# Hybrid DeltaNet and attention layer: compact diagonal blocks, unit blocks set by GpSimd, X stored in two parts, separate places for the out weights, later planned landings

## The chip, the cores and the metric

The kernel runs on one NeuronCore of a Trainium2 chip. The core has five engines with a queue each, which run in order and wait for one another by semaphores: TensorE (PE, with its weight loads shown as PEld), VectorE (DVE), ScalarE (ACT), GpSimd (POOL) and SyncE (SP), from which this kernel issues all its DMA transfers. The metric is the device time of one execution, in microseconds; less is better.

## What is computed

One layer of an encoder over 2048 positions of width 1024. The normalised input is projected once; the columns are split between a bidirectional gated DeltaNet of 4 heads of 128 and windowed attention of 8 query heads of 64. Both results are joined, multiplied by the output weights and added to the input. The DeltaNet part, cut to what the change touches:

```python
k_beta = k * beta[..., None]
m = jnp.where(strict, jnp.einsum('bhncd,bhnsd->bhncs', k_beta, k) * decay, 0.0)
eye = jnp.eye(c, dtype=q.dtype)
t_inv = lax.linalg.triangular_solve(eye + m, jnp.broadcast_to(eye, m.shape),
                                    left_side=True, lower=True, unit_diagonal=True)
u = jnp.einsum('bhncs,bhnse->bhnce', t_inv, v * beta[..., None])
w = jnp.einsum('bhncs,bhnsd->bhncd', t_inv, k_beta * jnp.exp(g)[..., None])
a_intra = jnp.where(incl, jnp.einsum('bhncd,bhnsd->bhncs', q, k) * decay, 0.0)
...
fwd = gated_delta_rule_chunked(q, k, v, g[:, :, 0], beta[:, :, 0])
bwd = flip(gated_delta_rule_chunked(flip(q), flip(k), flip(v), flip(g[:, :, 1]), flip(beta[:, :, 1])))
...
mix = jnp.concatenate([dn, sw], axis=-1).astype(x.dtype)
x = x + mix @ w_out[l].astype(x.dtype)
```

The kernel works with 16 chunks of 128 positions, where the reference has 32 of 64; the result is the same. All is in float32; the large products are made of three float32r products of a high and a low part.

## The kernel before

**Phase A** (`phase_a`) projects the input. For the second half of the positions it holds the x blocks 2 and 3 in the pools `xp0` and `xp1` and ends with the gates z (matmuls `pf_z`, first of block 2, then of block 3). Its pools stand on the right side of the on-chip memory in the order bp, xp0, xp1, wp, zp. Intermediate results go to DRAM tiles: `kq_d`, `v_d`, `zdn_d`, `mix_sw`.

**Phase B** (`phase_b`) runs the DeltaNet heads 0 to 3 one after the other, each in four steps.

1. `pre_front(h)`, by groups of four chunks (in the order 1, 2, 0, 3): k and q are loaded (L619) and transposed; `gh` (L656) is k·k and q·k. For both directions d, DVE multiplies by beta and the decay (L665) into `ma` [128, 4, 2, 128]: index 0 of the third axis is M (the strict triangle), index 1 is the intra-chunk matrix A. Both go in one DMA of 512 KB to the DRAM tile `m_d` (L670). POOL adds the two directions' M to `wm` (L672, called W below), which holds the lower triangle of one direction and the upper of the other.
2. `pre_back(h)`, first part: the 32x32 diagonal blocks of M of both directions (16 chunks, 4 blocks each, 128 blocks in all, one on each partition) are read from `m_d` into `L0` and `L` (L697, L698); `X` is loaded with unit blocks from the input `eye32` (L699). DVE turns L0 into L (L700) and inverts the blocks in 31 steps of two small operations (L704, L708), which is called the solve. X is stored to `x_d` in one DMA (L709).
3. `pre_back(h)`, second part: `spread` loads X by groups (`xc`, L757), transposes it (L758) and writes it with `own` as block-diagonal matrices `ut` and `tt` (L761, DVE and POOL). Products with `wm` (`za`, `ra`, `zb`, `rb`, L720) complete the inverse in `tt`.
4. `scan(h)`: 16 steps in each direction. A step loads `at` (A, from `m_d`, L781) and `kqc` (L784), and its chain is pk (L785), r (L787), py (L793), yk (L798), pn (L802), the new state S (L805). The output of a step is py times `at` and the like (L811). After step 12 and at the end `post` normalises, gates and stores to `mix_dn`.

In program order `pre_front(1)`, then scan 0, `pre_back(1)`, `pre_front(2)`, scan 1, and so on. Between them stand the matmuls of the attention half of the output projection (`out_half` with names in s, `pcs`, L566 to L568), which depend only on `mix_sw` and on the lower half of the output weights. Their result is stored to `part_d`. The upper half of the weights is loaded after scan 3, for the matmuls `pcd`, which add `part_d` and x (`xr`, `x2`, L561 to L570) and write the output.

`load_wo` loads a half of the output weights in eight pieces of 256 KB to a staging tile (L542), makes the high part on ACT (L543) and the low part on DVE (L544). Before the change both halves use the same tiles `woh` and `wol` of the pool `ww`. Staging tiles have the tag "ws" with two buffers, which `out_half` also uses. The pools of phase B on the right side stand in the order kv1, tp0, wo, ww, tp1, rp, kv2, over the places of bp, xp0, xp1 and wp; a pool may be used when all users of the places under it are done.

**The order of the work** is not that of the program. `set_order` takes all instructions, gives each a duration (`cost`) and each DMA a time to landing (`landing`), plans the queues of all five engines by list scheduling, forwards and backwards, tries 120 changed orders, and fixes the best by its own estimate. So any changed instruction or estimate gives a new order for the whole kernel, and each engine keeps to it, also where a transfer lands later than planned.

Of the kernel before, what the change touches and what calls it, by code (L numbers as in the profile page):

```python
# [8 lines left out]
F32 = mybir.dt.float32  # L9
# [7 lines left out]
P = 128  # L17
# [12 lines left out]
def tile_hybrid(ctx, tc, t, out, dbg=None):  # L30
# [16 lines left out]
    nw = const("nw", [P, KC], t["nwt"])  # L47
    bd = const("bd", [P, NCH, 16])
# [8 lines left out]
    with ExitStack() as ca:  # L57
        consts = phase_a(ca, tc, t, ident, nw, bd, gp, mix_sw, kq_d, v_d, zdn_d, zsw_d, dp)
# [6 lines left out]
def phase_a(ctx, tc, t, ident, nw, bd, gp, mix_sw, kq_d, v_d, zdn_d, zsw_d, q_pool):  # L65
# [15 lines left out]
    def const(name, shape, src=None):  # L81
        a = ap.tile(shape, F32, tag=name, name=name)
        if src is not None:
            dma(a, src)
        return a

    cw = gp.tile([P, 12, 5], F32, tag="cw", name="cw")
    dma(cw, t["cw"])
# [8 lines left out]
    edge = gp.tile([P, 12, 4], F32, tag="edge", name="edge")  # L97
# [420 lines left out]
def phase_b(ctx, tc, t, ident, consts, hp, mix_dn, mix_sw, kq_d, v_d, zdn_d, zsw_d, dp, out):  # L518
# [28 lines left out]
    def out_half(pool, bank, w, mx, srcs, dst, name, nb):  # L547
# [36 lines left out]
    with tc.using_default_side("right"):  # L584
        right = {n: pool(n, 2 if n == "wo" else 1) for n in 'kv1 tp0 wo ww'.split()}
    late = ctx.enter_context(ExitStack())
    with tc.using_default_side("right"):
        ps_s = pool("ps_s", stack=late, space=PSUM)
        right.update({n: pool(n, 2 if n == "rp" else 1, late) for n in 'tp1 rp kv2'.split()})
    kvp += [right["kv1"], right["kv2"]]  # L590
    tp = [right["tp0"], right["tp1"]]
    wo, ww, rp = right["wo"], right["ww"], right["rp"]
# [10 lines left out]
    def pre_front(h):  # L603
# [9 lines left out]
        m_d = dp.tile([2, NCH, 4 * (64 * P + 32)], F32, tag=f"m_d{h}", name=f"m_d{h}")  # L613
        x_d = dp.tile([2, NCH, P, 32], F32, tag="x_d", name=f"x_d{h}", bufs=2)
        for n, c4 in enumerate(FRONT):
# [53 lines left out]
            for d in range(2):  # L669
                dma(m_d[d, s4, : 2 * P * P].rearrange("u (i y) -> i u y", y=2 * P), mas[d].rearrange("p u a n -> p u (a n)"))  # L670
            wm[c4] = qp.tile([P, 4, P], F32, tag="wm", name=f"wm{h}_{c4}", bufs=7)
            G.tensor_tensor(wm[c4], mas[0][:, :, 0], mas[1][:, :, 0], ALU.add)  # L672
            tr = ps_t.tile([P, 4, P], F32, tag="tr", name=f"trv{h}_{c4}")
# [9 lines left out]
        H["solve"] = m_d, x_d  # L683
        return H

    def pre_back(h, H):
        wm, tt = H["wm"], H.setdefault("tt", {})
        m_d, x_d = H["solve"]
# [6 lines left out]
        lv = [m_d[d].rearrange("u (p y) -> (u p) y", p=4)[:, : 64 * P] for d in range(2)]  # L695
        lv = [a.rearrange("q (r x) -> q r x", x=2 * P)[:, :, :32] for a in lv]
        dma(L0, lv[0])  # L697
        dma(L[64:128], lv[1])  # L698
        dma(X, t["eye32"].partition_broadcast(P))  # L699
# [9 lines left out]
        dma(x_d.rearrange("d u (p r) c -> (d u p) (r c)", p=4), X.rearrange("p r c -> p (r c)"))  # L709
# [57 lines left out]
    def scan(h, H, rp, ps_s):  # L767
        ks, vs, ck, tt = (H[k] for k in ("ks", "vs", "ck", "tt"))
        m_d = H["solve"][0]
        oacc = H["oacc"] = {}  # L770
        st = {}
        for i in range(NCH):
            for d in range(2):
# [7 lines left out]
                dma(at, m_d[d, c, : 2 * P * P].rearrange("(i a j) -> i a j", a=2, j=P)[:, 1])  # L781
# [75 lines left out]
    ws = load_wo(wo, 4, "s")  # L857
# [35 lines left out]
def set_order(tc):  # L893
# [367 lines left out]
```

## Time and profile before

| | us |
|---|---|
| runs of before (3) | 1288.22, 1292.0, 1293.46 |
| median | 1292.0 |
| the profiled execution, its own time | 1291.88 |
| its span, first to last instruction | 1290.1 |
| head 0: solve, first step to store of X | 757 to 800 |
| head 1: solve | 847 to 913 |
| head 2: solve | 946 to 1016 |
| head 3: solve | 1043 to 1084 |
| scans 0 to 3, first S to last S | 837 to 920, 945 to 1031, 1049 to 1130, 1122 to 1201 |
| attention half of the output, first to last pcs | 805 to 1143 |
| last half of the output, first to last pcd | 1183 to 1286 |

The stages overlap: while one head is scanned, DVE solves the next one and PE runs the front of the one after. The profile is that of one execution, and all times in it count from its first instruction. Its rows are shown below, where they are used.

### The profile page before, as it was taken

The page shows a single profiled execution, that of the slowest core. Times are in us where ns is not written, and L with a number is a line of the kernel's source. Part 1 is how long each engine was busy: PE and PEld are TensorE (multiplying, and loading weights), DVE is VectorE, ACT ScalarE, POOL GpSimd, SP SyncE. Part 2 cuts the span into 40 slices and gives each one's busy share as a digit, 9 for nine tenths or more (in the row PEclk, how much of TensorE's full clock was granted, in tenths as well). Part 3 has the DMA queues.
Part 4 walks back from the last instruction along what each step waited for, and adds up shares of the span by engine and source line. Part 5 has one row for each costly group of instructions (what it writes and reads, how often), then busy time and mean ns, then how long its engine had stood idle before and what let it go on. Part 6 is the DMA issues. An engine that isn't in the chain of part 4 may idle for free.

```text
span 1290.1 us, 22274 instructions
## 1 busy us (share of the span) xinstructions
PE 1220.2 (95%) x7034; PEld 1043.6 (81%) x7034; DVE 939.1 (73%) x2346; ACT 700.8 (54%) x2057; POOL 486.3 (38%) x606
## 2 busy tenths in 40 slices
PE   4999999999999999999999999699999999998998
PEld 4998878888899987787778877587788788986776
DVE  4312477777888778799997878789779888766443
ACT  5322254435677777877755455476566655555211
POOL 1330214104667677886312313512422320213333
PEclk9999999999999999999999999799999999999999
DMA  8453244325542344421247567878868765378897
GB/s 259 129 144 104 82 145 146 119 86 173 162 123 81 113 117 135 137 88 67 74 146 265 177 175 240 221 190 256 236 158 255 248 160 159 100 230 272 250 309 227
DMA packets 238519, 218.01 MB, mean 169 GB/s; under 512 B 50624, under 2 KB 189632, under 8 KB 238400
## 3 DMA queue, kind: packets, MB, share of 16 engines
q1 hardware_dynamic: 238400, 216.58, 55.4%
q8 instruction: 56, 0.92, 0.3%
q14 instruction: 63, 0.52, 0.1%
HBM read 143.05 MB, written 73.47 MB: 168 GB/s over the span
## 4 chain that ended last, share of the span: by engine, by line
PE 75%; DMA 10%; DVE 6%; ACT 4%; issue 2%; SPq 2%; POOL 1%; DVEq 0%; ACTq 0%; POOLq 0%
PE pf_c L188 6%; PE pf_c L189 6%; PE pf_c L190 6%; PE pf_z L189 3%; PE pf_z L188 3%; PE pf_z L190 3%; PE pt L362 3%; PE pq_q L199 2%; PE pq_q L200 2%; PE pq_q L201 2%; PE pcs L566 2%; PE pcd L567 2%; PE gh L656 2%; PE pcs L567 2%; PE pk L793 2%
## 5 line engine op out<-in xcount | busy, mean ns | idle before, releaser
L239 DVE SCALAR_TENSOR_TENSOR acc<-pf_c,cw,acc 128x512 f32<-128x512 f32 (+2 forms) x192 | 140.6, 745 | 28.1 <-ACT acc L235 22.7
L188 PE MATMUL pf_c<-xhi,wh_c 128*128 128x512 f32 x384 | 150.8, 401 | 1.1 <-DVE acc L239 0.9
L189 PE MATMUL pf_c<-xlo,wh_c 128*128 128x512 f32 x384 | 151.6, 401 | 0.0
L190 PE MATMUL pf_c<-xhi,wl_c 128*128 128x512 f32 x384 | 149.5, 400 | 0.0
L357 POOL TENSOR_SCALAR pr<-pr,st 128x384 f32<-128x384 f32 (+1 forms) x128 | 84.6, 681 | 62.9 <-DVE st L355 32.4
L189 PE MATMUL pf_z<-xlo,wh_z 128*128 128x512 f32 x256 | 100.3, 404 | 0.0
L188 PE MATMUL pf_z<-xhi,wh_z 128*128 128x512 f32 x256 | 99.9, 404 | 0.0
L190 PE MATMUL pf_z<-xhi,wl_z 128*128 128x512 f32 x256 | 99.7, 402 | 0.0
L348 ACT ACTIVATE pr<-pr,st 128x384 f32<-128x384 f32 (+1 forms) x128 | 76.1, 596 | 21.3 <-DVE st L347 18.2
L188 PEld LDWEIGHTS pf_c<-xhi,wh_c 128*128 128x128 f32 x384 | 72.3, 188 | 16.8 <-DVE acc L239 1.6
L189 PEld LDWEIGHTS pf_c<-xlo,wh_c 128*128 128x128 f32 x384 | 72.2, 188 | 14.7
L190 PEld LDWEIGHTS pf_c<-xhi,wl_c 128*128 128x128 f32 x384 | 72.1, 188 | 14.5
L367 DVE TENSOR_TENSOR pl<-pt,ph 128x512 fp32r<-128x512 f32 x92 | 62.2, 685 | 23.2 <-ACT ph L366 22.4
L563 POOL TENSOR_TENSOR xrd<-xrd,x2d 128x512 f32<-128x512 f32 x32 | 42.3, 1324 | 95.9 <-DMA x2d<-x 35.3
L343 DVE CUSTOM_DVE_ANT_0 pr<-s,mask,sink 128x384 f32<-128x384 f32 (+1 forms) x128 | 73.4, 593 | 6.4 <-PE s L342 4.5
L362 PE MATMUL pt<-ident,pr 128*128 128x128 f32 x368 | 71.0, 275 | 2.3 <-POOL pr L357 1.0
L366 ACT ACTIVATE ph<-pt 128x512 fp32r<-128x512 f32 x92 | 53.7, 594 | 33.5 <-PE pt L362 27.1
L199 PE MATMUL pq_q<-wh_q,xhi 128*128 128x256 f32 x256 | 69.0, 289 | 0.8 <-ACT sgq L258 0.8
L200 PE MATMUL pq_q<-wh_q,xlo 128*128 128x256 f32 x256 | 69.5, 285 | 0.0
L201 PE MATMUL pq_q<-wl_q,xhi 128*128 128x256 f32 x256 | 68.2, 284 | 0.0
L798 ACT ACTIVATE yk<-pk,ck 128x128 f32<-128x128 f32 x120 | 44.1, 368 | 38.8 <-PE pk L793 38.1
L566 PE MATMUL pcs<-wohs,mhs 128*128 128x512 f32 x128 | 57.5, 449 | 6.0 <-ACT wohs L543 4.2
(251 smaller groups left out, 3775.1 us busy)
## 6 DMA issues: line engine op xcount, KB each, us to landing
m_d<-ma SPq DMA_DIRECT2D x32, 512.0 KB, 4.9
kqc<-kq_d SPq DMA_DIRECT2D x120, 128.0 KB, 3.3
ws_c<-wt SPq DMA_DIRECT2D x48, 256.0 KB, 3.4
xr<-x SPq DMA_DIRECT2D x16, 512.0 KB, 5.9
ws_z<-wt SPq DMA_DIRECT2D x32, 256.0 KB, 3.7
kq<-kq_d SPq DMA_DIRECT2D x16, 512.0 KB, 5.5
at<-m_d SPq DMA_DIRECT2D x128, 64.0 KB, 2.9
part<-xrs SPq DMA_DIRECT2D x32, 256.0 KB, 3.2
```

What stands on the lines that cost most here:

```text
L188: T.matmul(ps, hi[:, k, cs], xhi[b][:, k], start=(k == 0), stop=False)
L189: T.matmul(ps, hi[:, k, cs], xlo[b][:, k], start=False, stop=False)
L190: T.matmul(ps, lo[:, k, cs], xhi[b][:, k], start=False, stop=(k == KC - 1))
L199: T.matmul(ps[:, :n], xh, hi[:, k, :n], start=(k == 0), stop=False)
L200: T.matmul(ps[:, :n], xl, hi[:, k, :n], start=False, stop=False)
L201: T.matmul(ps[:, :n], xh, lo[:, k, :n], start=False, stop=(k == KC - 1))
L239: V.scalar_tensor_tensor(av, ps[:, lo:], cw[:, i, k : k + 1], av, ALU.mult, ALU.add)
L343: V.tensor_tensor_reduce(pr[j][:, :n], ps[:, :n], mask[:, lo * P : hi * P], 1.0, sink[:, hh : hh + 1], ALU.add, ALU.max, accum_out=mx[:, j ...
L348: A.activation(pr[j][:, :n], pr[j][:, :n], AF.Exp, bias=nm[:, j : j + 1], accum_out=den[:, j : j + 1])
L357: G.tensor_scalar(pr[j][:, :n], pr[j][:, :n], den[:, j : j + 1], 1.0, ALU.mult, ALU.mult)
L362: T.transpose(pt[:, j], pr[j][:, (kb - lo) * P : (kb - lo + 1) * P], ident)
L566: T.matmul(ps, mh[:, k], wh[:, k, ns], start=(k == 0), stop=False)
```

## The change

- `pre_front`: only A goes to DRAM, to the tile `a_d` (256 KB a DMA in place of 512). W is made by POOL as before; then four ACT copies take its four diagonal 32x32 blocks to `lc` [128, 4, 32], which is stored compactly to `l_d` (64 KB a group).
- `pre_back`: L0 and L are both read from `l_d`, 4 KB in a row for each partition, where they were 32 rows of 128 bytes each from `m_d`. Each reads both triangles and the solve uses one. The unit blocks are set by two memsets on POOL; the input `eye32` is gone. X is stored in two DMAs, rows 0 to 23 and rows 24 to 31 of each block.
- `scan`: `at` is read from `a_d`.
- Pools: on the right side now kv1, wo, wwh, wwl, tp0, then tp1, rp, kv2. The high and the low part of the first half of the weights have a pool each. Their staging goes round five buffers of `wo` (tags ws, ml, ws, ml, mh). The second half has its own pool `op`, on the left side after `pre_stack` is closed, and its load stands before scan 3 in program order. `oc`, with the buffers of the last output stage, moves to the right side after `wo`, `wwh`, `wwl` and `tp0` are closed; x2 has four buffers in place of two.
- The constants nw, bd, cw and edge, used in phase A only, go to a pool of phase A.
- `set_order`: issues of `at` and `kqc` are planned with 630 ns (450 or 560 before), and every DMA lands 700 ns later in the plan.

```diff
-    def load_wo(pool, k0, name, tg=""):
-        wh = ww.tile([P, 4, D], F32R, tag="woh" + tg, name=f"woh{name}", bufs=1)
-        wl = ww.tile([P, 4, D], F32R, tag="wol" + tg, name=f"wol{name}", bufs=1)
+    def load_wo(pools, k0, name, stage):
+        wh, wl = (p.tile([P, 4, D], F32R, tag=n, name=f"{n}{name}", bufs=1) for p, n in zip(pools, ("woh", "wol")))
...
-                sw = pool.tile([P, 512], F32, tag="ws", name=f"wos{name}_{k}_{j}")
+                sw = stage(2 * k + j)
...
-                x2 = pool.tile([P, 512], F32, tag="x2", name=f"x2{name}_{j}", bufs=2)
+                x2 = pool.tile([P, 512], F32, tag="x2", name=f"x2{name}_{j}", bufs=4)
...
-        right = {n: pool(n, 2 if n == "wo" else 1) for n in 'kv1 tp0 wo ww'.split()}
+        kvp.append(pool("kv1"))
+        outs = ctx.enter_context(ExitStack())
+        wo = pool("wo", 2, outs)
+        ww = [pool(n, stack=outs) for n in ("wwh", "wwl")]
+        tp = [pool("tp0", stack=outs)]
...
-        m_d = dp.tile([2, NCH, 4 * (64 * P + 32)], F32, tag=f"m_d{h}", name=f"m_d{h}")
+        l_d = dp.tile([NCH, P, 32], F32, tag="l_d", name=f"l_d{h}", bufs=2)
+        a_d = H["a_d"] = dp.tile([2, NCH, P, P], F32, tag=f"a_d{h}", name=f"a_d{h}")
...
-                dma(m_d[d, s4, : 2 * P * P].rearrange("u (i y) -> i u y", y=2 * P), mas[d].rearrange("p u a n -> p u (a n)"))
+                dma(a_d[d, s4].rearrange("u i y -> i u y"), mas[d][:, :, 1])
             wm[c4] = qp.tile([P, 4, P], F32, tag="wm", name=f"wm{h}_{c4}", bufs=7)
             G.tensor_tensor(wm[c4], mas[0][:, :, 0], mas[1][:, :, 0], ALU.add)
+            lc = qp.tile([P, 4, 32], F32, tag="lc", name=f"lc{h}_{c4}", bufs=2)
+            for q in quads:
+                A.activation(lc[q], wm[c4][q, :, q], AF.Copy)
+            dma(l_d[s4].rearrange("u i c -> i u c"), lc)
...
-        lv = [m_d[d].rearrange("u (p y) -> (u p) y", p=4)[:, : 64 * P] for d in range(2)]
-        lv = [a.rearrange("q (r x) -> q r x", x=2 * P)[:, :, :32] for a in lv]
-        dma(L0, lv[0])
-        dma(L[64:128], lv[1])
-        dma(X, t["eye32"].partition_broadcast(P))
+        lv = l_d.rearrange("u (p r) c -> (u p) r c", p=4)
+        dma(L0, lv)
+        dma(L[64:128], lv)
+        xf = X.rearrange("p r c -> p (r c)")
+        G.memset(xf, 0.0)
+        G.memset(xf[:, ::33], 1.0)
...
-        dma(x_d.rearrange("d u (p r) c -> (d u p) (r c)", p=4), X.rearrange("p r c -> p (r c)"))
+        xs = x_d.rearrange("d u (p r) c -> (d u p) r c", p=4)
+        for rs in (slice(0, 24), slice(24, 32)):
+            dma(xs[:, rs], X[:, rs])
...
-                dma(at, m_d[d, c, : 2 * P * P].rearrange("(i a j) -> i a j", a=2, j=P)[:, 1])
+                dma(at, H["a_d"][d, c])
...
-    ws = load_wo(wo, 4, "s")
+    def stage(i):
+        tag, bufs = (("ws", 2), ("ml", 2), ("ws", 2), ("ml", 2), ("mh", 1))[i % 5]
+        return wo.tile([P, 512], F32, tag=tag, name=f"wos{i}", bufs=bufs)
+
+    ws = load_wo(ww, 4, "s", stage)
...
     ps3 = pool("ps3", space=PSUM)
+    op = pool("op")
+    with tc.high_priority(-1000000):
+        w = load_wo((op, op), 0, "d", lambda i: op.tile([P, 512], F32, tag="wt", name=f"wod{i}", bufs=2))
     scan(3, H, rp3, ps3)
     late.close()
+    outs.close()
     with tc.using_default_side("right"):
         ps_c = pool("ps_c", 4, space=PSUM)
-    oc = pool("oc", 8)
-    with tc.high_priority(-1000000):
-        w = load_wo(wo, 0, "d")
+        oc = pool("oc", 8)
...
-            return 450 if dims < 2 else 560
+            return 630 if o[0].tensor.name.startswith(("at", "kqc")) else 450 if dims < 2 else 560
...
-            return 1800 + n / (450 if sum(c > 1 for _, c in o.ap) < 3 else 190)
+            return 2500 + n / (450 if sum(c > 1 for _, c in o.ap) < 3 else 190)
...
-        return 1900 + n / 190 + 1000 * any(t == 0 for t, _ in a.ap) + 1200 * (run < 64)
+        return 2600 + n / 190 + 1000 * any(t == 0 for t, _ in a.ap) + 1200 * (run < 64)
```

More of the change, by code (lines that the diff above doesn't have):

```diff
@@ L57, in tile_hybrid @@
     with ExitStack() as ca:
-        consts = phase_a(ca, tc, t, ident, nw, bd, gp, mix_sw, kq_d, v_d, zdn_d, zsw_d, dp)
+        consts = phase_a(ca, tc, t, ident, gp, mix_sw, kq_d, v_d, zdn_d, zsw_d, dp)
     with ExitStack() as cb:
@@ L62, in tile_hybrid, with phase_a @@
         dbg(tc, locals())
-def phase_a(ctx, tc, t, ident, nw, bd, gp, mix_sw, kq_d, v_d, zdn_d, zsw_d, q_pool):
+def phase_a(ctx, tc, t, ident, gp, mix_sw, kq_d, v_d, zdn_d, zsw_d, q_pool):
     nc = tc.nc
@@ L79, in phase_a, with const @@
     pso = ctx.enter_context(tc.tile_pool(reuse_waits="tile", name="pso", bufs=1, space=PSUM))
-    def const(name, shape, src=None):
-        a = ap.tile(shape, F32, tag=name, name=name)
+    def const(name, shape, src=None, pool=ap):
+        a = pool.tile(shape, F32, tag=name, name=name)
         if src is not None:
@@ L85, in const @@
         return a
-    cw = gp.tile([P, 12, 5], F32, tag="cw", name="cw")
-    dma(cw, t["cw"])
+    nw = const("nw", [P, KC], t["nwt"], zp)
+    bd = const("bd", [P, NCH, 16], None, zp)
+    cw = const("cw", [P, 12, 5], t["cw"], zp)
     mask = const("mask", [P, 3 * P], t["smask"])
@@ L96, in phase_a @@
     sink = const("sink", [P, NQ], t["sinks"].partition_broadcast(P))
-    edge = gp.tile([P, 12, 4], F32, tag="edge", name="edge")
+    edge = const("edge", [P, 12, 4], None, zp)
     half_neg = const("half_neg", [P, 16])
@@ L588, in phase_b @@
         ps_s = pool("ps_s", stack=late, space=PSUM)
[L589 to L592, printed above, removed]
+        tp.append(pool("tp1", stack=late))
+        rp = pool("rp", 2, late)
+        kvp.append(pool("kv2", stack=late))
     XE = V
@@ L681, in pre_front @@
             V.tensor_tensor(ck[:, d], bp[:, d], ekd[:, d, :, h], ALU.mult)
-        H["solve"] = m_d, x_d
+        H["solve"] = l_d, x_d
         return H
@@ L687, in pre_back @@
         wm, tt = H["wm"], H.setdefault("tt", {})
-        m_d, x_d = H["solve"]
+        l_d, x_d = H["solve"]
         L0 = qp.tile([P, 32, 32], F32, tag="kq", name=f"L0{h}", bufs=2)[:64]
```

5 lines of the change are left out of this document (1 added, 4 removed).

## The prediction

> **What bounds the kernel now.** I read the page first, then the busy time of each engine by stage (stages cut at the first and last instruction of each head's solve and scan), then the SP queue's timeline, the DMA issues, the waits and the chain that ended last.
>
> ```profile
> span 1290.1 us, 22274 instructions
> PE 1220.2 (95%) x7034; PEld 1043.6 (81%) x7034; DVE 939.1 (73%) x2346; ACT 700.8 (54%) x2057; POOL 486.3 (38%) x606
> ```
>
> PE looks full, and the change takes no matmul away. So all that can be won is time in which PE stands still or waits for a chain. By stage (columns: stretch, its length, busy us and count of PE, PEld, DVE, ACT, POOL, then granted clock, DMA share, GB/s):
>
> ```profile
> 734.00:757.00 23.00, 20.59 (x94) 16.37 (x92) 18.17 (x27) 11.60 (x30) 3.91 (x3) 1.00 0.72 183
> 757.00:800.00 43.00, 41.89 (x196) 34.06 (x197) 38.04 (x98) 22.39 (x95) 11.05 (x9) 0.96 0.71 221
> 800.00:834.00 34.00, 22.60 (x105) 18.61 (x105) 23.40 (x48) 12.93 (x39) 18.42 (x13) 0.80 0.89 240
> 847.00:913.00 66.00, 62.05 (x407) 54.08 (x406) 56.26 (x188) 45.64 (x196) 19.63 (x15) 0.97 0.79 225
> 913.00:945.00 32.00, 27.30 (x174) 23.15 (x173) 26.17 (x57) 17.83 (x63) 15.48 (x10) 1.00 0.87 231
> 945.00:1016.00 71.00, 70.13 (x469) 62.44 (x469) 62.27 (x204) 50.16 (x207) 17.84 (x14) 0.98 0.71 212
> 1016.00:1049.00 33.00, 30.53 (x197) 26.78 (x196) 27.37 (x72) 17.47 (x59) 14.25 (x10) 1.00 0.79 218
> 1122.00:1182.00 60.00, 52.97 (x391) 47.90 (x390) 42.60 (x140) 39.38 (x167) 12.66 (x9) 0.97 0.77 234
> 1182.00:1290.00 108.00, 98.02 (x428) 76.07 (x428) 46.42 (x90) 20.27 (x62) 36.44 (x27) 1.00 0.81 260
> sum 590.00, PE 544.31 PEld 463.98 DVE 438.04 ACT 301.21 POOL 173.97; mean PE 41.87 PEld 35.69 DVE 33.70 ACT 23.17 POOL 13.38
> ```
>
> From 700 us to the end PE is idle 590 − 544.3 = 45.7 us. The largest hole, 34 − 22.6 = 11.4 us, lies between the end of head 0's solve (800) and its scan (834). Then come the same turn of head 1 (913 to 945, 4.7 us) and of head 2 (1016 to 1049, 2.5 us), scan 3, which has little other work beside it (7.0 us), and the tail (10 us). In the long stretches between, DVE is busy 85% (56.26 of 66) and 88% (62.27 of 71): there it, not PE, is close to being the bound. What PE waited for by name:
>
> ```profile
> PE tr L636 <- DMA kq<-kq_d: 7.6, 4, 3.1
> PE pza L720 <- DVE ut L761: 7.0, 2, 5.6
> PE pcs L566 <- ACT wohs L543: 4.2, 1, 4.2
> PE pk L785 <- DMA kqc<-kq_d: 2.7, 4, 1.0
> ```
>
> All four belong to parts that the change touches: a load held up, the spread of the solved blocks, the out weights, a load of the scan.
>
> **The change part by part.** Steps on the path are told by these issues (size, then median us from issue to landing):
>
> ```profile
> m_d<-ma SPq DMA_DIRECT2D x32, 512.0 KB, 4.9
> ws_c<-wt SPq DMA_DIRECT2D x48, 256.0 KB, 3.4
> at<-m_d SPq DMA_DIRECT2D x128, 64.0 KB, 2.9
> q_d<-sgq SPq DMA_DIRECT2D x32, 128.0 KB, 1.8
> L<-m_d SPq DMA_DIRECT2D x8, 256.0 KB, 5.6
> X<-eye SPq DMA_DIRECT2D x4, 512.0 KB, 6.0
> x_d<-X SPq DMA_DIRECT2D x4, 512.0 KB, 3.8
> xc<-x_d SPq DMA_DIRECT2D x32, 64.0 KB, 2.9
> ```
>
> *A. Compact diagonal blocks, head 0.* The SP queue before head 0's solve, and the copy that opens the solve (first of four):
>
> ```profile
> 737.78 0.47 SPq L670 DMA_DIRECT2D m_d<-ma  x1
> 746.06 0.62 SPq L698 DMA_DIRECT2D L<-m_d  x1
> 748.33 0.60 SPq L697 DMA_DIRECT2D L<-m_d  x1
> L700 DVE COPY L<-L x4: 1021/1052/1103, 754.6 to 1041.4; 64x1024 f32<-64x1024 f32 x4
> ```
>
> From the last store of M to the solve's first instruction pass 754.6 − 737.8 = 16.8 us, and for 746.06 − 738.25 = 7.8 us of them SP issues nothing: the read of L waits at its head for the store to land, and the loads behind it are late too. Afterwards the path is: W on POOL, four ACT copies of a 32x32 block column, a 64 KB store, two reads of 256 KB. POOL and ACT by these rows:
>
> ```profile
> L672 POOL TENSOR_TENSOR wm<-ma,ma x16: 1273/1300/2807, 684.7 to 1046.3; 128x512 f32<-128x512 f32 x16
> L741 ACT ACTIVATE tt<-pra x16: 268/268/273, 823.5 to 1114.0; 32x128 f32<-32x128 f32 x16
> L847 ACT ACTIVATE oacc<-oacc,sso 128x128 f32<-128x128 f32 x64 | 20.8, 400 | 3.0 <-POOL sso L840 2.8
> ```
>
> No 32-row copy from SBUF is in the trace: it lies between 268 ns (same form, from PSUM) and 400 ns (128 rows, with a scale); I take 300, being nearer the first. The store of 128-byte runs is not there either: between 1.8 us (128 KB store in longer runs) and 4.9 (the store of M); I take 2.5, as it has an eighth of M's bytes. The reads now have 4 KB runs; bounds 3.4 (256 KB of weights) and 5.6 (today's); I take 3.7. Sum: 1.3 + 1.2 + 2.5 + 0.9 (two issues) + 3.7 = 9.6 us, and I add 2.5 for standing in three queues: 12, against 16.8. That is **−4.5 us** (bounds −8 and +2), and it counts in full, since all that follows to 834 hangs on this solve and PE's filler then is still plentiful (41.9 of 43 busy to 800).
>
> In the sum above the short runs cost little, because 64 KB in 128-byte runs (the loads of xc) lands in 2.9 us and 64 KB in 512-byte runs (at) in 2.9 too. The Trainium skill ("DMA: Bandwidth & Descriptors", Specifications) speaks against this part: below 512 B a transfer is not at line rate, since it is read, modified and written. By that rule the l_d store would be the slow kind, near M's 4.9 us, and A would shrink to about −2 (a forecast of 1276); the equal 2.9 us, of loads though, speak for the smaller price.
>
> *B. Unit blocks on POOL.* The 512 KB read of the identity (6.0 us) goes; two memsets of POOL come. No memset of that size is in the trace; POOL's 128x512 add with two inputs takes 1.3 us, so 1024 elements without an input cost between nothing and 2.6 us, and I take 1.5. It runs while L is still loading, hence 0; were it late, 1.5 a head. DMA traffic falls by 8.4 MB (M without its diagonal half), 2.1 (identity), and rises by 1 (l_d).
>
> *C. Heads 1 to 3.* The same shorter path, but the solve there is filler on a DVE that is 85 to 88% busy, so most of an earlier start is lost again: **−1 each, −3** (0 to −9).
>
> *D. X stored in two parts.* Rows 0 to 23 are final eight steps before the end and go out beside them; what is left at the end is 128 KB, 1.8 us by q_d instead of 3.8 for 512 KB. It is seen at head 0, where the 5.6 us wait for ut is this latency, and at heads 1 and 2, where the chain names it:
>
> ```profile
> 821.28 5.78 DMA woss<-wout
> 842.03 4.27 DMA woss<-wout
> 1016.36 4.67 DMA x_d<-X
> 1162.16 5.01 DMA wosd<-wout
> ```
>
> I count 1.5, 1.5 and 1, and 0.5 for head 3, whose turn scan 2 covers: **−4.5** (−8 to 0).
>
> *E. Places for the out weights.* Before, woh and wol share one pool over both x blocks' place, with two staging buffers:
>
> ```profile
> L543 ACT ACTIVATE wohs<-woss x8: 617/626/630, 804.7 to 846.3; 128x512 fp32r<-128x512 f32 x8
> L543 ACT ACTIVATE wohd<-wosd x8: 629/630/634, 1158.6 to 1190.2; 128x512 fp32r<-128x512 f32 x8
> ```
>
> So the first half arrives from 804.7 to 847, and the chain shows its loads at 821 and 842: PE has no filler in just the hole where it wants it. With the high part over the first x block alone and five staging buffers, five of eight pieces can stand ready at 805 and the rest land some 6 us later. The 4.2 us wait goes, with some of the small holes after 813; but the filler used here is missing later: **−4** (0 to −10). The second half gets its own place and need not wait for the last sw matmul: its 8 × 0.63 us of ACT, and as much DVE, leave scan 3's last steps, and the 5 us load at 1162 leaves the chain. Scan 3 and the start of the tail have 7 + 10 us of holes; I take **−3** (0 to −7). x2 with four buffers lies in the same tail and is in that number.
>
> *F. What it costs.* 64 ACT copies, 64 × 0.3 = 19 us (17 to 26) on an ACT that is 69% busy (45.64 of 66) in its worst stage, and in order: the scan's yk and y stand behind them. Most is hidden by ACT's idle third; I take **+3** (0 to +16, the rival below). SP gets 16 + 4 − 4 more issues of about 0.4 us, hidden by shorter reads of L.
>
> *G. Later planned landings.* The order is planned again with loads and stores taken 0.7 us longer. Today's 2.9 for at is over the old plan's (1.9 us, and one more for each 190 KB: 2.2) by just this. PE's two waits for loads are 7.6 + 2.7 = 10.3 us; I take a fifth, **−2** (−7 to +5: a new order of everything may fall out worse).
>
> Sum: −4.5 − 3 − 4.5 − 4 − 3 + 3 − 2 = **−18 us**. The profiled execution's span of 1290.1 belongs to a time of 1291.9, the median of the runs is 1292.0; so 1291.9 − 18 gives **1274 us**.
>
> **Granted clock, an upside not in the sum.** The holes go with a halved clock:
>
> ```profile
> 810.00:820.00 10.00, 5.71 (x18) 4.43 (x19) 7.59 (x12) 3.56 (x9) 7.35 (x5) 0.59 0.95 292
> 820.00:830.00 10.00, 5.82 (x35) 5.39 (x35) 6.52 (x19) 2.90 (x7) 3.49 (x3) 0.84 0.93 217
> 830.00:840.00 10.00, 9.70 (x67) 8.70 (x65) 8.01 (x14) 6.63 (x21) 5.73 (x4) 0.88 0.64 165
> ```
>
> The missing clock is 4.1 + 1.6 + 1.2 = 6.9 us; PE is idle for over half of the first two rows, so at most 3 us of work is lost to it. The Trainium skill ("TensorE: Matmul & The Clock Gate", The HAM clock gate) says that an idle window of about 3.4 us halves the clock until PE has been busy as long again; the rows agree. By it, filling the hole gives those 3 us on top.
>
> **The rivals.**
> 1. *DVE sets the pace* from 834 to 1122, and holes filled in one place open in another. For it: 85 and 88% of DVE, and no DVE instruction goes. Then C, D beyond head 0, and E's first half are worth nothing: −4.5 − 1.5 − 3 + 3 + 0 = −6, with G at 0 to +3: **1288**, no change that can be told. Against it: at 913 to 945 DVE has 5.8 us of holes itself, waiting for the blocks.
> 2. *ACT is held up by W* (slower). W was wanted late, at the inverse; now the copies wait on it in ACT's order, and what stands behind them (yk, y, exp of the next group) waits too. POOL's W takes 1.3 us, up to 2.8, and can stand behind another 1.3 us add. If each of the 16 groups keeps ACT 1.5 us beyond plan and 1.2 us of copies come on top, that is 43 us; with two thirds on the path +28, less the −18 − 3 of the other terms (F's +3 taken out): +7, **1299**. It decides from 21 / 16 = 1.3 us of path a group. Against it: ACT is idle 30% or more and the order plans for W.
> 3. *All holes close*: terms near their far ends, with the clock: about −35, **1257**. Needs DVE to give way, so unlikely.
>
> **How the numbers follow.** What a measurement of this kernel can tell from no change is about 0.5%, 6.5 us. Forecast (1262 to 1284) 0.61; rival 3 0.07; rival 1 0.18, nearly all of it within 0.5%; rival 2 0.14. Faster: 0.61 + 0.07 + a rest of rival 1 = 0.69; same 0.17; slower 0.14. The range for 8 in 10 leaves out the far half of rival 3 and most of rival 2: 1256 to 1297.
>
> **What would show it.** A: the store of l_d to the solve's copy in about 12 us for head 0, no SP pause near 8 us. D: last part of X to the first xc under 3 us. E: the sw half converted by about 815, the dn half before 1150 of the old clock, PE's wait for wohs gone. F: ACT busy 718 to 727 us, and no growing wait of ACT for POOL's W. Wrong would be: the holes after the solves as long as before (A, D fall), or PE's idle time unchanged in sum with the holes elsewhere (rival 1).

## The result: slower, where 18 us of gain were forecast

| | us |
|---|---|
| before, median of 6 runs | 1291.6 |
| after, median of 6 runs (1297.5 to 1305.5) | 1300.4 |
| forecast | 1274, range 1256 to 1297 |
| the profiled execution of after, its own time | 1300.95 |

The ratio after to before is 1.0077 with a 95% interval of 1.0053 to 1.0102: slower, and outside of the range. The first lines of the page of after:

```profile
span 1299.1 us, 22381 instructions
...
PE 1224.0 (94%) x7034; PEld 1041.1 (80%) x7034; DVE 945.9 (73%) x2346; ACT 723.8 (56%) x2121; POOL 489.5 (38%) x614
```

PE does the same work as before (1220.2 then) in a span 9 us longer. Busy time by stretch shows where it stands still. Before, with cuts at head 0's solve (757), its first state S (837) and scan 3's (1122); the columns are those of the prediction:

```profile
575.00:700.00 125.00, 122.32 (x618) 98.41 (x617) 113.30 (x285) 81.20 (x209) 49.59 (x71) 1.00 0.37 118
700.00:757.00 57.00, 54.59 (x249) 44.02 (x248) 45.83 (x76) 28.78 (x84) 14.79 (x12) 1.00 0.67 198
757.00:837.00 80.00, 67.45 (x320) 55.19 (x321) 64.38 (x150) 37.80 (x139) 31.20 (x23) 0.89 0.76 222
837.00:1122.00 285.00, 271.30 (x1830) 240.80 (x1830) 238.81 (x717) 174.98 (x655) 78.88 (x57) 0.99 0.70 198
```

And after, cut at the same events:

```profile
575.00:700.00 125.00, 118.12 (x599) 92.86 (x598) 113.37 (x287) 83.80 (x222) 59.38 (x84) 1.00 0.32 100
700.00:763.00 63.00, 63.00 (x289) 51.04 (x288) 56.57 (x95) 36.31 (x106) 16.41 (x17) 1.00 0.65 191
763.00:836.00 73.00, 67.40 (x363) 56.51 (x361) 62.45 (x151) 45.13 (x159) 31.12 (x24) 0.98 0.66 190
836.00:1119.00 283.00, 264.87 (x1737) 230.24 (x1737) 236.93 (x701) 180.72 (x675) 82.59 (x63) 0.98 0.64 182
1119.00:1186.00 67.00, 63.99 (x483) 59.34 (x483) 49.80 (x168) 45.62 (x184) 4.91 (x3) 1.00 0.66 195
1186.00:1299.00 113.00, 97.46 (x404) 74.63 (x404) 43.27 (x77) 18.64 (x58) 43.37 (x33) 0.98 0.80 270
```

The turn of head 0, which the change was to shorten, became shorter: 73 us in place of 80, the granted clock 0.98 in place of 0.89, PE idle for 5.6 us in place of 12.6. What got shorter is the solve (763 to 798, before 757 to 800). From its end to the first S it is 37 to 38 us in both (797.8 to 835.7, before 799.9 to 836.8), but PE's hole there fell from the 11.4 us of the prediction to 37 − 32.07 = 4.9, as more other matmuls stand in it:

```profile
798.00:835.00 37.00, 32.07 (x193) 27.98 (x192) 29.61 (x62) 24.97 (x84) 23.55 (x19) 0.95 0.74 187
```

But head 0's solve begins 6 us later (763 for 757), the stretch of scan 3 to the first pcd is 67 us long in place of 60, and the tail 113 in place of 108. The first of these losses lies in phase A, where no instruction of the change runs before 699 us, some constants of phase A that moved to another place aside: from 575 to 700 PE is idle 6.9 us (2.7 before), and POOL, which scales the attention's probabilities there, has 59.4 us of work in place of 49.6. What PE waits for in after, by name:

```profile
PE pcd L565 <- DVE mld L553: 11.2, 9, 2.3
PE pt L361 <- POOL pr L356: 5.9, 8, 1.7
...
PE pza L729 <- DVE ut L770: 3.0, 3, 1.7
```

The waits of before are smaller (ut, 7.0 then) or off this list (kq, wohs); new are the transposes of probabilities, in phase A (5.9 us; before 1.0), and the last half of the output (11.2; 2.6).

**A finer measure.** Busy shares hide queueing and a slower clock, so I worked out the time that PE loses. Each PE instruction gets a floor: the distance to the next start among instructions of the same tiles and form in the trace of before, as the median of the shorter half. The lost time up to t is t less the floors of all that started before t. In total it moves with the span.

| PE time lost, us | before | after | difference |
|---|---|---|---|
| 0 to 700 | 82.8 | 94.6 | +11.8 |
| 700 to 775 | 6.0 | 1.4 | −4.6 |
| 775 to 850 | 22.3 | 12.7 | −9.6 |
| 850 to 1175 | 43.1 | 45.4 | +2.3 |
| 1175 to the end | 17.9 | 27.1 | +9.2 |

So 14 us were won around head 0's turn, and 21 lost: ahead of it and in the tail.

### The profile page after: what moved, and what is told of

It is laid out like the page before. It is cut to its first block, busy times and chain, and to the rows that moved or that the text cites. A ratio compares the mean times of both kernels' runs of the same rounds, so it can differ in the third digit from the quotient of the medians.

```text
span 1299.1 us, 22381 instructions
## 1 busy us (share of the span) xinstructions
PE 1224.0 (94%) x7034; PEld 1041.1 (80%) x7034; DVE 945.9 (73%) x2346; ACT 723.8 (56%) x2121; POOL 489.5 (38%) x614
## 5 line engine op out<-in xcount | busy, mean ns | idle before, releaser
L238 DVE SCALAR_TENSOR_TENSOR acc<-pf_c,cw,acc 128x512 f32<-128x512 f32 (+1 forms) x192 | 139.2, 745 | 24.4 <-ACT acc L234 18.0
L356 POOL TENSOR_SCALAR pr<-pr,st 128x384 f32<-128x384 f32 (+1 forms) x128 | 89.0, 712 | 90.7 <-DVE st L354 50.5
L188 PE MATMUL pf_z<-xlo,wh_z 128*128 128x512 f32 x256 | 96.7, 402 | 0.0
L189 PE MATMUL pf_z<-xhi,wl_z 128*128 128x512 f32 x256 | 96.2, 400 | 0.0
L361 PEld LDWEIGHTS pt<-ident,pr 128*128 128x128 f32 x368 | 47.3, 141 | 25.7 <-POOL pr L356 12.4
L806 ACT ACTIVATE yk<-pk,ck 128x128 f32<-128x128 f32 x120 | 43.9, 368 | 42.8 <-PE pk L801 41.0
```

What stands on the lines that cost most here:

```text
L188: T.matmul(ps, hi[:, k, cs], xlo[b][:, k], start=False, stop=False)
L189: T.matmul(ps, lo[:, k, cs], xhi[b][:, k], start=False, stop=(k == KC - 1))
L238: V.scalar_tensor_tensor(av, ps[:, lo:], cw[:, i, k : k + 1], av, ALU.mult, ALU.add)
L356: G.tensor_scalar(pr[j][:, :n], pr[j][:, :n], den[:, j : j + 1], 1.0, ALU.mult, ALU.mult)
L361: T.transpose(pt[:, j], pr[j][:, (kb - lo) * P : (kb - lo + 1) * P], ident)
```

## The experiments

Two causes were weighed. One: the later planned landings (G of the prediction), which touch the order of everything, cost the time. The other: the places in memory (E) cost it, above all that of `oc`, which now waits for the first half of the weights to be used up. Beside both stood chance: each plan is searched with random changes, so any edit gives another order.

**1. The parts.** `old_landings` is the change with the durations and landings of the old plan:

```diff
-            return 630 if o[0].tensor.name.startswith(("at", "kqc")) else 450 if dims < 2 else 560
+            return 450 if dims < 2 else 560
...
-            return 2500 + n / (450 if sum(c > 1 for _, c in o.ap) < 3 else 190)
+            return 1800 + n / (450 if sum(c > 1 for _, c in o.ap) < 3 else 190)
...
-        return 2600 + n / 190 + 1000 * any(t == 0 for t, _ in a.ap) + 1200 * (run < 64)
+        return 1900 + n / 190 + 1000 * any(t == 0 for t, _ in a.ap) + 1200 * (run < 64)
```

> The changed kernel planned with the old landings and issue costs. Theory 'landings': the 12 us more of lost PE time that the changed kernel has by 700 us (94.6 against 82.8), where no instruction differs, come from planning with later landings. Expected: lost PE time at 700 us back to 81 to 85, time 1287 to 1292. Rival 'any new order scatters by this much': lost time at 700 us anywhere from 80 to 96, with no link to landings; time 1285 to 1305.

`landings_alone` is the kernel before with just the reverse of that diff:

> The kernel before, planned with the later landings and the dearer issues of at and kqc, nothing else changed. Theory 'landings': slower, 1299 to 1306, with 10 to 14 us more of PE time lost by 700 us. Rival, the step G of the prediction: loads are better met, 1286 to 1291. Rival 'scatter': within 6 us of 1291.6 on either side.

`blocks_alone` is the kernel before with l_d, a_d, the memsets and X in two parts (A, B, C, D, F), without the new places and landings:

> The kernel before with compact diagonal blocks from W, unit blocks by POOL and X in two parts, and nothing else: no new places, no later landings. Theory (steps A and D were right, the loss lies in places and landings): PE time lost between 700 and 850 us falls from 28 to about 15, lost time at 700 us stays 81 to 85, the tail stays as before; time 1276 to 1284. Rival 'ACT is held up by W': lost time between 850 and 1050 grows by 8 or more, time 1290 to 1300.

`oc_left` is the change with `oc` back on the left side:

```diff
-        oc = pool("oc", 8)
+    oc = pool("oc", 8)
```

> The changed kernel with one thing undone: the buffers of the last output stage (oc) stand on the left side again, so they may be filled when scan 2 is done, and need not wait for the last pcs. Theory 'place': in the changed kernel the first load of x comes at 1183 us (1148 before) because oc lies over the places of the first half of the weights, and the last stage is then paced by late loads (109 us from first to last pcd, 103.5 before; PE waits 11.2 us for mld). Expected: first x2 load before 1165, pcd stage 101 to 105 us, time 1289 to 1294. Rival 'the tail is paced by the order, whatever the place': pcd stage stays 107 or more, time 1297 to 1303.

| run | time | ratio to before |
|---|---|---|
| old_landings | 1277.3 | 0.9878 [0.9844, 0.9912] |
| landings_alone | 1307.3 | 1.0119 [1.0082, 1.0156] |
| blocks_alone | 1281.1 | 0.9911 [0.9880, 0.9943] |
| oc_left | 1287.2 | 0.9957 [0.9935, 0.9979] |

Without its later landings the change gains 15 us and comes out 3 us from the forecast; the later landings alone make the kernel before 15 us slower. `blocks_alone` gains 11 us by A, B, C, D and F, for which the prediction's sum has −9. But `oc_left` is 13 us faster than after, too, so the place of `oc` was still in play, though not by the shorter last stage that was expected: first to last pcd takes 111 us, and 109 in after. The profile of `old_landings`, by stretch (solve from 747, scan 0 from 823, pcd from 1164):

```profile
575.00:700.00 125.00, 121.10 (x612) 96.85 (x610) 113.73 (x280) 81.55 (x211) 51.17 (x70) 1.00 0.37 117
...
747.00:823.00 76.00, 70.90 (x382) 58.50 (x381) 66.66 (x157) 46.02 (x163) 28.96 (x23) 1.00 0.69 200
...
1164.00:1276.00 112.00, 100.49 (x426) 77.05 (x426) 44.29 (x85) 17.39 (x58) 43.85 (x33) 0.98 0.83 274
```

POOL's work after 575 is near that of before again (51.2 for 49.6), and PE is idle 3.9 us there in place of 6.9.

**2. Where the landings cost.** In two runs the order of phase A's instructions was held on all engines, as it stands in another kernel's plan; the rest was planned anew (`started` holds pairs of which the second may not begin before the first):

```diff
+    for e, names in held_order.items():
+        found = [at_key[e, x] for x in names if (e, x) in at_key]
+        for a, b in zip(found, found[1:]):
+            started[a].append(b)
```

`a_order_of_before` is after with the order of before in phase A, `a_order_of_after` the reverse.

> The changed kernel, in which the instructions of phase A keep the order among themselves that they have in the kernel before, on every engine; the plan (with the later landings) is free in all the rest and in how both are interleaved. Theory: the 12 us that the changed kernel loses more by 700 us come from the order of phase A that was planned with the later landings, and from nothing else in the change. Expected: lost PE time at 700 us 81 to 85 (94.6 in the changed kernel), time 1286 to 1292. Rival 'the moved constants or the new front of phase B disturb phase A whatever its order': lost time at 700 us stays over 90, time 1296 or more.

> The kernel before, in which the instructions of phase A keep the order that they have in the changed kernel; all else as before, planned with the old landings. Theory: that order alone costs about 12 us, lost PE time at 700 us 92 to 97, time 1300 to 1306. Rival: the loss needs something else of the change, lost time at 700 us 82 to 87, time 1289 to 1295.

`ocleft_oldland` joins the edits of `oc_left` and `old_landings`; `issue_cost_only` is `old_landings` with the 630 ns for issues of at and kqc put back:

> The changed kernel with two things undone: oc on the left side again, and the old landings and issue costs. Theory 'place and landings are two separate losses': below the 1277.3 of old landings alone by up to 8, 1268 to 1276, with lost PE time at 700 us 81 to 86. Rival 'oc mattered only because the later landings put the last pcs at 1176': 1275 to 1281.

> The changed kernel planned with the old landings, but with 630 ns for each issue of at and kqc. Theory: the loss is by the landings, so this stays near the 1277.3 of both undone, 1272 to 1283. Rival 'the dearer issues, SP being busy half its time in the scans, make the plan worse': 1288 to 1300.

| run | time | ratio to before |
|---|---|---|
| a_order_of_before | 1288.0 | 0.9967 [0.9952, 0.9982] |
| a_order_of_after | 1298.6 | 1.0047 [1.0026, 1.0068] |
| ocleft_oldland | 1277.4 | 0.9885 [0.9858, 0.9912] |
| issue_cost_only | 1276.7 | 0.9885 [0.9852, 0.9919] |

The order of phase A that was planned with the later landings is worth 7 to 12 us: taken out of after it gives 12.4 us back, put into before it costs 6.7. PE's lost time at 700 us says it more directly: 94.6 in after and 82.2 with the order of before, 82.8 in before and 93.3 with the order of after. So the moved constants, which stay moved in the first of these runs, are not the cause. The place of `oc` is worth nothing once the landings are the old ones (1277.4 for 1277.3). What `oc_left` had won was won by a new order under the later landings: 5.6 us of it lie before 700 us, where `oc` has no part, and 7.0 in the tail. The 630 ns for issues cost nothing.

**3. The size of the landings.** `landings_earlier` plans with landings 0.4 us shorter than the old ones (1400 and 1500), `loads_later` and `stores_later` with only the loads or only the stores 0.7 us later; the rest is `old_landings`.

> The changed kernel planned with landings 400 ns earlier than before (1400 and 1500 in place of 2500 and 2600), issue costs as before. Theory 'the plan was right before': the old plan's 450 ns of issue plus landing already met the measured times from issue to landing (3.7 planned, 3.4 to 3.6 measured for 256 KB of weights), so a wrong guess costs on this side too, by waits for data that is not there: 1281 to 1292. Rival 'earlier is better, since engines in order can only lose by waiting in the plan': 1265 to 1276. Rival 'scatter': 1272 to 1282.

> The changed kernel planned with the later landings for loads alone (2600), stores and issue costs as before. Theory 'every over-long landing costs': about half of the 23 us, 1285 to 1294, lost PE time at 700 us 86 to 91. Rival 'it is the round trips through DRAM, store and load': loads alone cost under 6 us, 1277 to 1283.

> The changed kernel planned with the later landings for stores alone (2500), loads and issue costs as before. Stores are the most overrated (128 KB of q: planned 3.2 with the later landing, 1.8 measured). Theory: 1284 to 1294, lost PE time at 700 us 86 to 92. Rival 'stores matter little as few wait for them': 1275 to 1281.

They took 1289.5 (0.9977 [0.9955, 0.9999]), 1294.3 (1.0017 [0.9998, 1.0036]) and 1293.0 (1.0013 [0.9990, 1.0036]). So each half costs 16 to 17 us in this draw and both together 23, which is not additive, and shorter landings cost 12 as well. Before 700 us PE loses 92.4 us with the later stores, 87.3 with the later loads and 85.0 with the shorter landings (`old_landings` 82.3). A direction alone ("later is worse") doesn't explain the times; either the old values are near the best, or the draw of `old_landings` is a lucky one. The next runs tell.

**4. How much is chance.** The search draws its changed orders from a seed:

```diff
-    rnd = random.Random(1)
+    rnd = random.Random(2)
```

With that (or 3) were run after, `old_landings`, the kernel before and `landings_alone`.

> The changed kernel, its random trials of orders begun from another seed: another order by the same plan. It measures scatter. Theory 'the landings cost, not the draw': 1294 to 1304, lost PE time at 700 us 91 to 97. Rival 'scatter of the draw': differs from 1300 by more than 8 us.

> The change without the later landings, second draw. Theory 'the landings cost 10 or more beyond the draw': 1272 to 1282, below every draw with later landings. Rival 'the draw': 1283 to 1296, among them.

> The change without the later landings, third draw. As for the second: theory 1272 to 1282, rival 1283 to 1296.

> The changed kernel, third draw. Theory: 1288 to 1302, above every draw with the old landings. Rival 'the draw': anywhere from 1275 on.

> The kernel before, second draw. Theory 'blocks and places are worth 10 to 18 us': the kernel before stays at 1286 to 1298 in another draw, above every draw of the change with the old landings. Rival 'the draw made the 15 us': 1275 to 1283.

> The kernel before with the later landings and issue costs alone, planned with the second draw of changed orders. Theory 1 (planning with the later landings costs some 13 us on average, whichever kernel it is put into and whichever draw): before with the second draw took 1288, so about 1301, and in any case over 1294. Theory 2 (the 15 us that the later landings cost in the kernel before were the bad luck of the first draw, since a changed plan scatters by up to 10 us): 1284 to 1294.

> The kernel before, nothing changed but the third draw of changed orders. It shows the scatter of the kernel before, where two draws gave 1292 and 1288. Theory 1 (the change without its later landings is worth some 9 us on average, with old landings 1277, 1279 and 1286): 1284 to 1296, mean of the three draws near 1290. Theory 2 (the change is worth nothing without the luck of a draw): some 1280, as the change with old landings.

| ratio to before by draw | 1 | 2 | 3 |
|---|---|---|---|
| before | 1 | 0.9962 ± 0.0022 | 1.0028 ± 0.0022 |
| before, later landings | 1.0119 ± 0.0037 | 1.0091 ± 0.0032 | |
| change, old landings | 0.9878 ± 0.0034 | 0.9887 ± 0.0038 | 0.9949 ± 0.0022 |
| change as it is | 1.0077 ± 0.0025 | 0.9990 ± 0.0015 | 0.9985 ± 0.0025 |

Of the last two runs, the later landings in before cost nearly what they cost in the first draw (1304.0 us, 1295.1 for before in a third draw), and before didn't come near the 1280 that pure luck would have given. A new draw alone moves a kernel by up to 0.9% (12 us), more than most terms of the prediction. The later landings cost time in all five pairs: 1.2 and 1.3% on before, 2.0, 1.0 and 0.4% on the change, 1.2% or 15 us in the mean. The rest of the change gains in all five: 1.2, 0.75 and 0.8% with the old landings, 0.4 and 1.0% with the later ones, 0.8% or 11 us in the mean. The draw of the change as it is was the worst of its three, that of `old_landings` the best of its three. So that the gain is lost is due to the later landings, but that the change came out slower is bad luck as well: in the other two draws it takes 1290.0 and 1290.4 us, as long as before and inside of the forecast's range. Two runs missed what was expected of them: `after_seed2` was put at 1294 or more, and `oldland_seed3`, with 1285.8, at 1282 or less.

PE's lost time, as means of these draws, shows where each part acts:

| us | before (3) | before, later (2) | change, old (3) | change as it is (3) |
|---|---|---|---|---|
| 0 to 700 | 87.5 | 97.7 | 81.0 | 90.5 |
| 700 to 775 | 4.1 | 2.0 | 2.4 | 2.8 |
| 775 to 850 | 19.0 | 18.4 | 15.9 | 13.5 |
| 850 to 1175 | 43.9 | 41.2 | 45.4 | 44.4 |
| 1175 to the end | 18.3 | 26.9 | 16.5 | 23.3 |

The later landings add 10 us before 700 and 7 to 9 in the tail, with the change and without it. The rest of the change takes 3 to 5 us from head 0's turn, where it was meant to, and some 7 before 700, where next to nothing of it runs; that second part is not explained.

## Why the prediction was wrong, point by point

**G is the step that failed.** It was put at −2 us, between −7 and +5; the runs give +15 in the mean of five pairs, and about 23 in the draw of the change. Its reason was that today's 2.9 us for at is over the old plan's 2.2 by just the 0.7 that is added. But the median of the profile counts from the issue, and the plan adds the landing to the issue's own 450 or 560 ns: 0.45 + 2.25 = 2.7 us by the old plan and 0.63 + 2.95 = 3.6 by the new one. The DMA issues of after:

```profile
kqc<-kq_d SPq DMA_DIRECT2D x120, 128.0 KB, 2.9
ws_c<-wt SPq DMA_DIRECT2D x48, 256.0 KB, 3.6
...
at<-a_d SPq DMA_DIRECT2D x128, 64.0 KB, 2.9
...
q_d<-sgq SPq DMA_DIRECT2D x32, 128.0 KB, 1.8
ql<-q_d SPq DMA_DIRECT2D x16, 256.0 KB, 3.0
```

Worked out in the same way (what the plan adds when transfers queue behind one another is left out), the old plan has 3.2, 3.7, 2.7, 2.5 and 3.7 us for these five, and the new one 3.9, 4.4, 3.6, 3.2 and 4.4. For these five the old plan was already within 0.2 us or late, by up to 0.7; the new one is late for all five, by 0.7 to 1.4. The rows of before (3.4, 2.9 and 1.8 us for ws_c, at and q_d) say the same. It is not so for every kind of transfer. For two loads of later stages both plans have the same numbers as for ws_c (3.7 and 4.4), and the new one meets the first and is still early for the second:

```profile
x2d<-x SPq DMA_DIRECT2D x32, 256.0 KB, 4.4
...
wos<-wout SPq DMA_DIRECT2D x8, 256.0 KB, 5.8
```

So the lateness fits phase A, and doesn't explain the loss in the tail, where x2d is loaded.

What a late plan does is seen in phase A. The attention's q goes to DRAM and back (q_d, then ql), turns on POOL, and feeds a chain of scores, probabilities and transposes. For a store and a load the new plan has 7.6 us, the old one 6.2 and the trace 4.8. The load ql (columns: shortest, median and longest issue, then first and last start) in before, in `old_landings`, in after and in `landings_alone_seed2`:

```profile
L311 SPq DMA_DIRECT2D ql<-q_d x16: 319/360/505, 82.8 to 568.7; - x16
```

```profile
L310 SPq DMA_DIRECT2D ql<-q_d x16: 319/380/848, 84.6 to 568.3; - x16
```

```profile
L310 SPq DMA_DIRECT2D ql<-q_d x16: 319/324/459, 85.2 to 577.2; - x16
```

```profile
L311 SPq DMA_DIRECT2D ql<-q_d x16: 319/382/487, 88.8 to 583.1; - x16
```

With the old landings the last q is fetched at 566 to 573 us in the three draws of either kernel; with the later ones at 573 to 583 in all five. By 300 us 12 to 15 of the 368 transposes of probabilities have run with the old landings in all three draws of before and of `old_landings`, and 8 in these five with the later ones. So the plans push the attention back, and more of its chain falls at the end of phase A; with that goes POOL's 59.4 us of work after 575. PE's wait for `pr` is no sure mark of it: it is 4.3 and 4.4 us in the other two draws of before. The later stores alone bring 8 transposes by 300 us and 10.1 of the 12.3 us that PE loses more before 700, which fits the store of q as the most overrated of the five.

That the order of phase A carries the cost is shown by the held orders; that it is the lateness of this store and load in the plan which pushes the attention back is argued. The lost time doesn't follow the delay closely: `oc_left`, planned with the later landings, has 16 transposes by 300 us and loses 89.0 us by 700, and `after_seed2` has 8 and loses 86.6, less than two draws of before (88.7 and 91.0). How the later landings cost time in the tail is open. Why landings 0.4 us shorter cost 12 us too stays open as well; that was run in one draw only.

**A was right.** The SP queue of after ahead of head 0's solve, and the copy that opens it:

```profile
749.50 0.42 SPq L678 DMA_DIRECT2D l_d<-lc  x1
749.98 0.50 SPq L672 DMA_DIRECT2D a_d<-ma  x1
754.00 0.49 SPq L702 DMA_DIRECT2D L<-l_d  x1
754.54 1.00 SPq L703 DMA_DIRECT2D L<-l_d  x1
...
760.31 1.11 DVE L707 COPY L<-L 64x1024 f32<-64x1024 f32 x1
```

From the last store to the copy it is 10.8 us (forecast 12, before 16.8), and SP's pause is 754.0 − 750.5 = 3.5 us in place of 7.8. These are not like intervals, as the store comes later in the new path, and the sum of 12 begins with W. From the last W of head 0 to the copy it is 14.4 us (745.9 to 760.3), and 20.4 before (734.2 to 754.6): 6.0 us saved, where 4.5 were forecast. The parts of the sum were less good. The issues of after:

```profile
L<-l_d SPq DMA_DIRECT2D x8, 256.0 KB, 4.2
...
x_d<-X SPq DMA_DIRECT2D x4, 384.0 KB, 2.8
...
l_d<-lc SPq DMA_DIRECT2D x16, 64.0 KB, 4.3
...
x_d<-X SPq DMA_DIRECT2D x4, 128.0 KB, 3.6
```

The store of l_d takes 4.3 us, not 2.5, and lies near the other bound (4.9). The rule that I weighed against this part, that runs under 512 B are slow (the Trainium skill, "DMA: Bandwidth & Descriptors", Specifications), is not decided by that: single stores of l_d, in runs of 128 B, took 1.8 to 6.9 us, and the four last parts of X, twice as large and in runs of 1 KB, 1.8 to 5.3. Nor did the 2.5 us allowed for queues cover it: the sum was 2.3 us short, and A kept its size because the way of before was longer by the same measure.

**B was right.** The second read of L is issued at 754.5; the first memset starts at 753.4 and takes 0.95 us, with the second 1.1 in all (1.5 taken). It is done long before the copy:

```profile
L705 POOL MEMSET X<- x4: 951/953/956, 753.4 to 999.7; 128x1024 f32 x4
L706 POOL MEMSET X<- x4: 152/158/166, 754.4 to 1001.9; 128x32 f32 x4
```

**C is not seen in the time.** The solves of heads 1 and 2 shrink from 66 and 70 us to 43 and 47, but scan 3 begins 283.7 us after scan 0 (1119.4 − 835.7), before 285.5: 1.8 us of more than 20 are kept (forecast 3). And PE's lost time from 850 to 1175, where these heads stand, did not fall: it rose by 2.3 us in this draw, and by 1.5 and 3.2 in the means. That an earlier start of filler is mostly lost again, as the prediction said, fits this.

**D failed at head 0.** The store of X, or of its last part, to the first read of X in before:

```profile
799.89 0.33 SPq L709 DMA_DIRECT2D x_d<-X  x1
...
803.30 1.00 SPq L757 DMA_DIRECT2D xc<-x_d  x1
```

and in after:

```profile
797.78 0.32 SPq L718 DMA_DIRECT2D x_d<-X  x1
798.19 0.52 SPq L621 DMA_DIRECT2D kq<-kq_d  x1
799.44 0.38 SPq L672 DMA_DIRECT2D a_d<-ma  x1
799.87 1.24 SPq L631 DMA_DIRECT2D dc<-gr_d  x2
801.20 3.29 SPq L766 DMA_DIRECT2D xc<-x_d  x4
```

It is 3.4 us in both (forecast under 3). The last 128 KB landed in 1.8 us here, as forecast, but other issues stood ahead of the read in SP's order until 801.2. And the 512 KB of before had landed in 2.6 us at this head, not in the median of 3.8. Elsewhere the smaller part was no faster: it took 5.3 and 4.9 us at heads 1 and 2, where the 512 KB of before took 5.3 and 4.7, and in `old_landings` 4.0 us at head 0, with the read waiting for it. So the time is not in the bytes, and 1.8 from q_d was no price for it: q_d, 128 KB in runs of 1 KB as well, is stored in phase A, where the DMA engines are less busy (share 0.33 to 0.42 by stretches of 100 us from 100 to 600 in before, 0.66 to 0.76 over head 0's turn). That this load is the reason is argued. The wait for ut fell all the same, from 7.0 to 3.0 us.

**E failed in its times.** The conversions of the weights in after:

```profile
L541 ACT ACTIVATE wohs<-wos x8: 615/618/630, 796.8 to 844.3; 128x512 fp32r<-128x512 f32 x8
...
L541 ACT ACTIVATE wohd<-wod x8: 614/620/650, 1164.5 to 1191.0; 128x512 fp32r<-128x512 f32 x8
```

The first half is not there at 815 but at 844, as before (846), and the first pcs runs at 845 (805 before); the hole after the solve closed with other matmuls (363 of all kinds in the stretch, 320 before). The second half is converted no earlier than before (1158.6 to 1190.2), since the plan doesn't put it earlier; in `old_landings` it is done at 1157. The tail loses less on average (18.3 to 16.5 us, and 26.9 to 23.3 with the later landings), but three draws of before alone lie between 15.1 and 22.0, so that a gain of 3 us is not told from chance. As a whole E is what `old_landings` has over `blocks_alone`: 3.8 us (1277.3 and 1281.1) of 7 forecast, in one draw and less than draws scatter. The new place of `oc`, where x2 has its four buffers, delays its loads instead. First loads of x2d in before, after and `old_landings`:

```profile
L562 SPq DMA_DIRECT2D x2d<-x x32: 327/382/997, 1148.1 to 1279.6; - x32
```

```profile
L560 SPq DMA_DIRECT2D x2d<-x x32: 333/428/760, 1183.6 to 1277.5; - x32
```

```profile
L560 SPq DMA_DIRECT2D x2d<-x x32: 328/410/761, 1161.5 to 1256.9; - x32
```

On the right side `oc` stands over the first half's weights, so in after no load of the last stage begins before the last pcs (1176.6): 35 us later than before. With the old landings this costs nothing that can be measured.

**F was right.** ACT is busy 723.8 us (718 to 727 forecast), and a copy takes 307 ns (300 taken):

```profile
L677 ACT ACTIVATE lc<-wm x64: 290/307/312, 701.1 to 1036.2; 32x128 f32<-32x128 f32 x64
...
  POOL wm L674: 7.0, 6
```

The second row is ACT's idle time ahead of these copies until W came: 7.0 us in all, where the second rival needed 16 × 1.5 = 24. In `blocks_alone` PE's lost time from 850 to 1050 grew by 2.9 us, where this rival wanted 8 or more. It forecast the right sign, at 1299, but was not the cause. Nor was the first, DVE: the loss is ahead of DVE's long stages and behind them. Without G the forecast was −16 us; the runs give −11 in the mean and −5 to −16 by draw. G hid it.

**The faster version** is the change with the old landings: 1277.3 us, ratio 0.9878 [0.9844, 0.9912], and 1278.8 and 1285.8 in two other draws. It beats both kernels in each.

## What to carry over

Before a planner's estimate is changed, compare like with like: the whole of what the plan adds from issue to use, against the same interval in the trace, for each kind of transfer. An edit that makes a whole schedule new has a scatter of its own (here up to 1%), so its parts are judged over several draws, and its loss can lie far from the edited lines. A stretch that doesn't contain a changed instruction is the first place to look when local gains are visible and the total is not.

## What the hardware showed that was not expected

The granted clock was halved for about 10 us although PE had no long pause. Busy time of after in two stretches of 10 us, then PE's timeline there (in brackets the idle time ahead):

```profile
870.00:880.00 10.00, 7.38 (x46) 5.84 (x44) 10.00 (x29) 4.28 (x16) 3.41 (x3) 1.00 0.89 262
880.00:890.00 10.00, 8.46 (x28) 6.90 (x29) 8.75 (x32) 2.56 (x10) 1.59 (x3) 0.51 0.32 100
```

```profile
878.51 0.49 PE L803 MATMUL po<-S,kqc 128*128 128x128 f32 x2 [1.17 <-DVE oacc L830]
```

The longest pause from 870 to 890 is this one of 1.17 us; PE was merely busy 74% with short matmuls, and for 1.6 of the last 3.4 us ahead of the halving at 880.2. The Trainium skill ("TensorE: Matmul & The Clock Gate", The HAM clock gate) ties the halving to an idle window of about 3.4 us; here it came without one, after sparse work. It cost some 3 us of PE time (an estimate: 128x128 matmuls took 421 ns in it and 275 outside, so about a third of the 8.46 us busy) in a stretch that has no output matmuls to fill it.
